# A hybrid decoder layer on one core: additions moved behind the next step, loads reordered at the ends of column pairs

## The chip, the cores and the metric

One core of a Trainium2 chip runs the whole program. The metric is the time of one execution in microseconds on the device: the median of the runs, before the change 1211.42 us over three (1210.86 to 1213.59). The core's engines are TensorE (PE in the profile), VectorE (DVE), ScalarE (ACT), GpSimd (POOL) and SyncE (SP). Each has its own queue of instructions, which it works off in order; semaphores tie the queues together. DMAs are issued from the queues of SyncE, GpSimd and ScalarE and carried out by 16 DMA engines.

## The reference, cut to what matters

256 tokens and 16 meta tokens in front of them go through one layer of width 2048. It has two halves, a mixer and a feed-forward block, and only the second is touched by the change:

```python
h = h + mix                                      # mixer: retention and mLSTM heads, then w_out
u = rmsnorm(h, norm_ffn)
up = causal_dwconv(u @ w_up, ffn_conv_w, ffn_conv_b)   # 2048 -> 2 x 5632, three taps
gate, val = jnp.split(up, [FFN_DIM], axis=-1)
h = h + (silu(gate) * val) @ w_down              # 5632 -> 2048
h = rmsnorm(h, norm_final)
return h[:, N_META:]
```

Everything is float32.

## The kernel before

**Products in three parts.** Each matrix operand is split into a rounded part `hi` (ScalarE's copy) and a rest `lo` (VectorE's subtraction, raw minus hi), and a product is hi·hi + hi·lo + lo·hi. So each raw weight tile costs one ScalarE copy (L141, L768), one VectorE subtraction (L143, L770) and three matmuls per pair of operands. Five `whi` and five `wlo` buffers stand between the splits and TensorE.

**Weights.** Raw weight tiles come through four buffers, `wraw0` and `wraw1` with two each (`raw_home`, L119). The loads of the mixer and the up-projection go round through them by a counter (`load_raw`, L122): two loads to side 0, two to side 1. The loads of the down-projection name their side themselves and do not move the counter.

**The feed-forward block** runs in two halves of the hidden width (from L759 on). A half has 44 up-projections (176 weight loads over both halves), the convolution, the gate, and then its part of the down-projection, summed into `hn`, the output tile of two token blocks `tt` of 128 rows by four column blocks `b` of 512.

**The down-projection of a half** takes the four column blocks as two pairs, `b` = 0 and `b` = 2. A pair has 11 steps `q`, each over 256 hidden rows. Steps 0, 9 and 10 are plain (`product`): two weight tiles, 24 matmuls of 512 columns. Steps 1 to 8 are fast (`seven`, L826): a scheme of seven products for a 2 by 2 block, 21 matmuls. Its raw tile of four quarters is in `left`, two buffers in the memory of `hT`, used in turn. VectorE forms one difference tile `ta` from it (L832); a precomputed sum `tb` comes by a load of its own. Both have their places in two buffers of `wraw1` (`sums_home`). Then four groups are split and multiplied. The quarter `raw[:, 0]` and the sum are read from `kept`, which was made in DRAM by accumulating DMAs (`Early`) during the up-projection.

In the last pair (second half, `b` = 2; `final`) three of the fast steps are done as plain ones, the order is 0, 1, 6, 2, 7, 3, 4, 5, 8, 9, 10, and the last normalization is woven in: `squares` on ScalarE, `times_gain` on GpSimd with the gain vector `gfin`, paced by a small GpSimd instruction (L855) that reads the step's sum.

**The end of a pair.** At the last fast step (8), `share` (L867 to L884) combines the four shared accumulators and adds the results to `hn`: GpSimd issues four accumulating DMAs (`onto`), to blocks (0, b), (1, b), (0, b+1), (1, b+1) in this order, and the last of them is `shared`. After step 10, four more accumulators `cs` are copied by ScalarE to tiles `x` (L1003) and added by VectorE to the same blocks of `hn` (L1004), after the DMA to the block has landed. The last of those copies is `emptied`; the splits of the next pair's first fast step are queued behind it.

**Order.** The framework draws up each engine's queue ahead of time: of what is ready at a moment, the work that comes first in the program. `issue_after(i)` puts work behind instruction `i` on that engine's queue, without waiting for it to end. SyncE's loads of the down-projection all go through `load` (L906), which chains them in program order by `begun`. GpSimd's sum loads are queued behind `shared`. At a pair's end SyncE's order is: step 8's tile, the next pair's step 1 (asked for at step 7), step 10's plain tiles, the next pair's step 0, its step 2 (both asked for at step 9).

Of the kernel before, what the change touches and what calls it, by code (L numbers as in the profile page):

```python
# [13 lines left out]
ALU = mybir.AluOpType  # L14
# [72 lines left out]
def trunk(ctx: ExitStack, tc: tile.TileContext, io, out: bass.AP):  # L87
# [28 lines left out]
    last_load = None  # L116
    loads = paced = 0

# [640 lines left out]
    for half in range(2):  # L759
# [66 lines left out]
        def seven(b, q, cs, ps, first, last, after, norm):  # L826
# [7 lines left out]
            for w, to in (  # L834
# [8 lines left out]
                with tc.issue_after(after.ins) if first and after else nullcontext():  # L843
                    copied, _ = split(hi[:, :n, :], lo[:, :n, :], w)
                for i, (m, o, begin, _) in enumerate(to):
# [4 lines left out]
            if norm:  # L850

                with tc.issue_after(copied.ins):
                    for g in norm:
                        squares(*g)
                reached = nc.gpsimd.tensor_tensor(out=junk[:, 0:1], in0=tb[:, 0, 0:1], in1=tb[:, 0, 0:1], op=ALU.add)  # L855
                with tc.issue_after(reached.ins):
                    for tt, _, c0, c1 in norm:
                        times_gain(tt, c0, c1)

        def block(tt, b):  # L860
# [41 lines left out]

        homes, raws = {}, {}
        begun = shared = None

# [10 lines left out]
        def load_seven(b, q):  # L916
# [9 lines left out]
        def load_sum(b, q):  # L926

            tb = sums_home[1][:, FAST.index(q) % 2, :][:, None, :]
            with tc.issue_after(shared.ins) if shared else nullcontext():
                nc.gpsimd.dma_start(tb[:, 0, :], early[b, half * NQD + q].kept[:, 1, :])  # L930
            homes[b, q] = homes[b, q], sums_home[0], tb
# [4 lines left out]
        lag = 4  # L936
        gains = []
        emptied = None
        for b in (0, 2):
# [18 lines left out]
            for q in steps:  # L958
                if q in fast:
                    due = []  # L960
                    if final and q != fast[0]:
                        due, gains = gains[:1], gains[1:]
                    seven(b, q, cs, ps, q == fast[0], q == fast[-1], emptied, due)
                    if q == fast[-1]:
# [18 lines left out]
                else:  # L983
# [5 lines left out]
                    if q == 8:  # L989
                        load_plain(b, 10, 1)  # L990
                    if b == 0:
                        if q == 7:
                            load_seven(2, 1)
                        elif q == 9:
                            load_plain(2, 0, 0)
                            load_seven(2, 2)
            for j in range(2):
                for n, tt in enumerate(range(2)):
                    c = (b + j) * 512
                    if not final:  # L1000

                        x = x_tile((4, 3, 1, 0)[2 * j + n])
                        emptied = nc.scalar.copy(x, cs[tt, j])  # L1003
                        nc.vector.tensor_tensor(out=block(tt, b + j), in0=block(tt, b + j), in1=x, op=ALU.add)  # L1004
                        if half == 1:
# [116 lines left out]
```

## Time and profile before

| | |
|---|---|
| median of three runs | 1211.42 us (1210.86 to 1213.59) |
| the profiled execution | 1212.01 us, its span 1210.2 us |
| TensorE busy | 1198.8 us, 99% |
| VectorE busy | 951.6 us, 79% |
| ScalarE busy | 713.4 us, 59% |
| DMA | 278.50 MB, mean 230 GB/s |
| first down-projection | TensorE from 718.8 to about 833.5 us |
| second down-projection | TensorE from 1087.2 us to the end |

Times in the views are microseconds from the span's start. A row of the timeline has the start, the length, the engine, the line, the operation, what it writes and reads, how many instructions it sums up, and in brackets how long the engine was idle before and what ended that. SPq and POOL rows of DMAs show the issue, not the transfer. Rows of the windows view have, per stretch, the stretch and its length, then for PE, PEld, DVE, ACT and POOL the busy time with the number of instructions that start or run in it, then the granted TensorE clock, the DMA engines' busy share and GB/s. Matmuls are pipelined, so the distance from start to start tells more than the length of one.

### The profile page before, as it was taken

The numbers are of one execution on the slowest core, as the hardware profiler recorded it, in microseconds if no ns is written. First come the engines' busy times: TensorE is split into PE (matmuls) and PEld (weight loads), VectorE is DVE, ScalarE is ACT, GpSimd is POOL, SyncE is SP. The second block draws the span as 40 slices with busy tenths as digits, with TensorE's granted clock in tenths as the row PEclk, the third lists the DMA queues.
The fourth block names the chain that finished last, engine by engine and source line by source line (L and its number), as shares of the span: only waits on it lengthen the run. The fifth ranks groups of instructions, "written<-read, shape, count | busy, mean of one in ns | idle before, by whom it ended". The sixth has DMA issues, their size and how long they took to land.

```text
span 1210.2 us, 23069 instructions
## 1 busy us (share of the span) xinstructions
PE 1198.8 (99%) x8947; PEld 1150.3 (95%) x8947; DVE 951.6 (79%) x1390; ACT 713.4 (59%) x973; POOL 258.7 (21%) x349
## 2 busy tenths in 40 slices
PE   9999999999999999999999999999999999999997
PEld 9999999999999999999999998878999999998786
DVE  8877778766775867788889779897877777778896
ACT  8657746656556556555555557665655555556673
POOL 0100022223231322233132100101133223300132
PEclk9999999999999999999999999999999999999999
DMA  7765677878786977788887757777888778847955
GB/s 278 263 224 159 203 235 210 254 217 238 209 244 208 260 223 222 238 256 227 237 229 224 233 181 261 229 249 228 271 228 252 240 222 237 221 161 265 291 195 183
DMA packets 102366, 278.50 MB, mean 230 GB/s; under 512 B 16432, under 2 KB 20656, under 8 KB 102128
## 3 DMA queue, kind: packets, MB, share of 16 engines
q1 hardware_dynamic: 84016, 239.06, 58.0%
q0 software_dynamic: 17664, 37.11, 17.5%
q8 instruction: 70, 1.15, 0.4%
q10 hardware_dynamic: 576, 0.85, 0.2%
q14 instruction: 40, 0.33, 0.1%
HBM read 268.59 MB, written 42.47 MB: 257 GB/s over the span
## 4 chain that ended last, share of the span: by engine, by line
PE 95%; DMA 2%; DVE 1%; ACT 0%; issue 0%; SPq 0%; DVEq 0%; ACTq 0%
PE mmps L150 25%; PE mmps L153 25%; PE mmps L151 25%; PE atps L821 2%; PE mmps L849 2%; PE atps L822 2%; PE atps L824 2%; PE mmps L846 2%; PE mmps L847 2%; PE atps L846 1%; PE atps L847 1%; PE atps L849 1%; DMA wraw<-in_wu 1%; DVE wlo L770 1%; DMA hT<-kept 1%; PE atps L444 1%
## 5 line engine op out<-in xcount | busy, mean ns | idle before, releaser
L141 ACT CAST whi<-wraw 128x1024 fp32r<-128x1024 f32 x346 | 361.8, 1049 | 334.0 <-PE mmps L151 221.6
L143 DVE TENSOR_TENSOR wlo<-wraw,whi 128x1024 fp32r<-128x1024 f32 x346 | 430.2, 1246 | 79.0 <-ACT whi L141 74.8
L150 PE MATMUL mmps<-uh,whi 128*128 128x258 f32 x1408 | 345.3, 283 | 0.6 <-ACT whi L141 0.6
L151 PE MATMUL mmps<-ul,whi 128*128 128x258 f32 x1408 | 345.0, 281 | 0.0
L151 PEld LDWEIGHTS mmps<-ul,whi 128*128 128x128 f32 x1408 | 266.6, 189 | 0.1
L150 PEld LDWEIGHTS mmps<-uh,whi 128*128 128x128 f32 x1408 | 265.3, 188 | 0.9 <-ACT whi L141 0.8
L150 PE MATMUL mmps<-xh,whi 128*128 128x272 f32 (+2 forms) x864 | 219.7, 287 | 0.0
L151 PE MATMUL mmps<-xl,whi 128*128 128x272 f32 (+2 forms) x864 | 218.2, 285 | 0.0
L153 PE MATMUL mmps<-uh,wlo 128*128 128x258 f32 x1408 | 197.9, 283 | 0.0
L153 PEld LDWEIGHTS mmps<-uh,wlo 128*128 128x128 f32 x1408 | 181.7, 189 | 0.0
L151 PEld LDWEIGHTS mmps<-xl,whi 128*128 128x128 f32 x864 | 162.6, 188 | 0.0
L150 PEld LDWEIGHTS mmps<-xh,whi 128*128 128x128 f32 x864 | 162.5, 188 | 0.1
L210 POOL TENSOR_TENSOR pace<-whi 128x1 f32<-128x1 f32 x87 | 52.2, 600 | 429.9 <-ACT whi L141 411.8
L153 PE MATMUL mmps<-xh,wlo 128*128 128x272 f32 (+2 forms) x864 | 126.8, 285 | 0.0
L153 PEld LDWEIGHTS mmps<-xh,wlo 128*128 128x128 f32 x864 | 114.5, 188 | 0.0
L697 DVE TENSOR_TENSOR cu<-mmps,rstd 128x258 f32<-128x258 f32 x88 | 37.6, 427 | 72.9 <-PE mmps L153 72.2
L770 DVE TENSOR_TENSOR wlo<-hT,whi 128x1024 fp32r<-128x1024 f32 x58 | 69.3, 1218 | 3.5 <-ACT whi L768 3.5
L768 ACT CAST whi<-hT 128x1024 fp32r<-128x1024 f32 x58 | 59.3, 1049 | 15.7 <-DMA hT<-kept 5.3
L768 ACT CAST whi<-wraw 128x1024 fp32r<-128x1024 f32 (+1 forms) x58 | 46.6, 835 | 35.5 <-DVE wraw L832 17.7
L151 PE MATMUL mmps<-mixl,whi 128*128 128x258 f32 x256 | 63.1, 283 | 0.0
L150 PE MATMUL mmps<-mixh,whi 128*128 128x258 f32 x256 | 62.5, 283 | 0.0
L770 DVE TENSOR_TENSOR wlo<-wraw,whi 128x1024 fp32r<-128x1024 f32 (+1 forms) x58 | 53.2, 952 | 1.5 <-ACT whi L768 0.5
(272 smaller groups left out, 1768.3 us busy)
## 6 DMA issues: line engine op xcount, KB each, us to landing
wraw<-in_wu SPq DMA_DIRECT2D x176, 512.0 KB, 4.5
wraw<-in_wi SPq DMA_DIRECT2D x108, 512.0 KB, 4.5
wraw<-in_wo SPq DMA_DIRECT2D x32, 512.0 KB, 5.4
wraw<-in_wd SPq DMA_DIRECT2D x30, 512.0 KB, 5.6
kept<-in_wd SPq DMA_DIRECT2D x29, 512.0 KB, 6.8
kept<-in_wd POOLq DMA_DIRECT2D x58, 256.0 KB, 6.7
hT<-in_wd SPq DMA_DIRECT2D x29, 512.0 KB, 4.9
kept<-kept POOLq DMA_DIRECT2D x29, 256.0 KB, 5.4
```

The costliest lines, as they stand in the source:

```text
L141: nc.scalar.copy(hi, raw)
L143: nc.vector.tensor_tensor(out=lo, in0=raw, in1=hi.bitcast(F32), op=ALU.subtract)
L150: nc.tensor.matmul(ps, hi[:, k, :], xh(kk), start=kk == first, stop=False)
L151: nc.tensor.matmul(ps, hi[:, k, :], xl(kk), start=False, stop=False)
L153: nc.tensor.matmul(ps, lo[:, k, :], xh(kk), start=False, stop=kk == last)
L210: with tc.issue_after(nc.gpsimd.tensor_tensor(out=pace, in0=x, in1=x, op=ALU.add).ins):
L697: evacuated = nc.vector.tensor_tensor(out=u, in0=ps[:, :NQ], in1=rstd2, op=ALU.mult)
L768: copied = nc.scalar.copy(hi, x)
L770: return copied, nc.vector.tensor_tensor(out=lo, in0=x, in1=hi.bitcast(F32), op=ALU.subtract)
L846: nc.tensor.matmul(o, sh[:, f, m, :], hi[:, i, :], start=begin, stop=False)
L847: nc.tensor.matmul(o, sl[:, f, m, :], hi[:, i, :], start=False, stop=False)
L849: nc.tensor.matmul(o, sh[:, f, m, :], lo[:, i, :], start=False, stop=end)
```

## The change

Six edits, all but one in the down-projection:

1. The additions of `cs` to column block `b + 1` at the end of each half's first pair are not made there: they are put on a list and made behind the next pair's first fast step. Those to block `b` and those of the second pair stay.
2. The next pair's step 1 is no longer asked for at step 7, but at step 9 behind step 0's plain tiles. Its step 2, asked for there too, is issued by GpSimd, behind `shared`, and not by SyncE.
3. In the last pair the sums of steps 3 to 5 are loaded by SyncE through `load`.
4. `gfin` is loaded in four quarters at steps 3 to 6 of the second half's first pair, behind that step's sum load, and not as a whole when the down-projection begins.
5. The pacing instruction of GpSimd writes a scratch of its own, `pace`, in place of `junk`.
6. The counter of the weight loads starts at 3 in place of 0, so that the sides come in the order 1, 0, 0, 1, 1 and not 0, 0, 1, 1.

```diff
-    loads = paced = 0
+    loads, paced = 3, 0
...
-                    copied, _ = split(hi[:, :n, :], lo[:, :n, :], w)
+                    copied, parted = split(hi[:, :n, :], lo[:, :n, :], w)
...
-                reached = nc.gpsimd.tensor_tensor(out=junk[:, 0:1], in0=tb[:, 0, 0:1], in1=tb[:, 0, 0:1], op=ALU.add)
+                reached = nc.gpsimd.tensor_tensor(out=pace, in0=tb[:, 0, 0:1], in1=tb[:, 0, 0:1], op=ALU.add)
...
+            return parted
...
-            nc.gpsimd.dma_start(gfin, io["gfin"])
...
-            load(raw[:, 2:4, :], io["wd7"][b // 2, half * NQD + q][:, 2:4, :])
-            load(raw[:, 1, :], io["wd7"][b // 2, half * NQD + q][:, 1, :])
-            load(raw[:, 0, :], early[b, half * NQD + q].kept[:, 0, :])
+            w = io["wd7"][b // 2, half * NQD + q]
+            parts = ((raw[:, 2:4, :], w[:, 2:4, :]), (raw[:, 1, :], w[:, 1, :]), (raw[:, 0, :], early[b, half * NQD + q].kept[:, 0, :]))
+            for to, src in parts:
+                if (b, q) == (2, 2):
+                    with tc.issue_after(shared.ins):
+                        nc.gpsimd.dma_start(to, src)
+                else:
+                    load(to, src)
...
-            with tc.issue_after(shared.ins) if shared else nullcontext():
-                nc.gpsimd.dma_start(tb[:, 0, :], early[b, half * NQD + q].kept[:, 1, :])
+            kept = early[b, half * NQD + q].kept[:, 1, :]
+            if half == 1 and b == 2 and q > 2:
+                load(tb[:, 0, :], kept)
+            else:
+                with tc.issue_after(shared.ins) if shared else nullcontext():
+                    summed = nc.gpsimd.dma_start(tb[:, 0, :], kept)
...
-                    seven(b, q, cs, ps, q == fast[0], q == fast[-1], emptied, due)
+                    done = seven(b, q, cs, ps, q == fast[0], q == fast[-1], emptied, due)
+                    if q == fast[0]:
+                        with tc.issue_after(done.ins):
+                            while later:
+                                later.pop(0)()
...
+                    if (half, b) == (1, 0) and q in range(3, 7):
+                        cols = slice((q - 3) * 512, (q - 2) * 512)
+                        with tc.issue_after(summed.ins):
+                            nc.gpsimd.dma_start(gfin[:, cols], io["gfin"][:, cols])
                     if b == 0:
-                        if q == 7:
+                        if q == 9:
+                            load_plain(2, 0, 0)
                             load_seven(2, 1)
-                        elif q == 9:
-                            load_plain(2, 0, 0)
                             load_seven(2, 2)
...
-                        nc.vector.tensor_tensor(out=block(tt, b + j), in0=block(tt, b + j), in1=x, op=ALU.add)
+                        later.append(lambda to=block(tt, b + j), x=x: nc.vector.tensor_tensor(out=to, in0=to, in1=x, op=ALU.add))
+                        if j == 0 or b == 2:
+                            later.pop(0)()
```

More of the change, by code (lines that the diff above doesn't have):

```diff
@@ L903, in trunk @@
         homes, raws = {}, {}
-        begun = shared = None
+        begun = shared = summed = None
         def load(to, src):
@@ L920, in load_seven @@
             turn = 1 - turn
-            load(raw[:, 2:4, :], io["wd7"][b // 2, half * NQD + q][:, 2:4, :])
-            load(raw[:, 1, :], io["wd7"][b // 2, half * NQD + q][:, 1, :])
-            load(raw[:, 0, :], early[b, half * NQD + q].kept[:, 0, :])
+            w = io["wd7"][b // 2, half * NQD + q]
[6 more added lines that the diff above has]
+                    load(to, src)
             homes[b, q] = raw
         def load_sum(b, q):
+            nonlocal summed
             tb = sums_home[1][:, FAST.index(q) % 2, :][:, None, :]
-            with tc.issue_after(shared.ins) if shared else nullcontext():
-                nc.gpsimd.dma_start(tb[:, 0, :], early[b, half * NQD + q].kept[:, 1, :])
+            kept = early[b, half * NQD + q].kept[:, 1, :]
[4 more added lines that the diff above has]
+                    summed = nc.gpsimd.dma_start(tb[:, 0, :], kept)
             homes[b, q] = homes[b, q], sums_home[0], tb
@@ L936, in trunk @@
         lag = 4
-        gains = []
+        gains, later = [], []
         emptied = None
```

## The prediction

> **What bounds the kernel now.** First the page's busy line and its slices, then TensorE (PE) by windows, its timeline where it is not steady, and the chain of waits there.
>
> ```profile
> span 1210.2 us, 23069 instructions
> PE 1198.8 (99%) x8947; PEld 1150.3 (95%) x8947; DVE 951.6 (79%) x1390; ACT 713.4 (59%) x973; POOL 258.7 (21%) x349
> 780.00:800.00 20.00, 20.00 (x87) 16.10 (x86) 19.94 (x21) 12.67 (x15) 2.16 (x4) 1.00 0.74 241
> 800.00:820.00 20.00, 19.03 (x78) 14.04 (x77) 18.05 (x18) 13.37 (x16) 1.08 (x2) 1.00 0.57 206
> ...
> 814.45 0.63 PE L849 MATMUL mmps<-wlo,sh 128*128 128x512 f32 x2
> 815.87 0.51 PE L846 MATMUL atps<-whi,sh 128*128 128x512 f32 x1 [0.79 <-ACT whi L768]
> ...
> 834.86 1.13 PE L153 MATMUL mmps<-uh,wlo 128*128 128x258 f32 x8
> 836.54 0.39 PE L150 MATMUL mmps<-uh,whi 128*128 128x258 f32 x1 [0.56 <-ACT whi L141]
> ...
> 1128.73 0.86 PE L849 MATMUL atps<-wlo,sh 128*128 128x512 f32 x3
> 1129.78 0.50 PE L846 MATMUL mmps<-whi,sh 128*128 128x512 f32 x1 [0.18 <-ACT whi L768]
> ...
> 807.71 8.29 DMA hT<-kept
> 826.73 8.63 DMA wraw<-in_wu
> ```
>
> TensorE is the bound: 1198.8 of 1210.2 us, at a granted clock of 1.00 in both windows. A change of this kind can only gain where TensorE waits, and in the stages it touches there are three such places. A steady 20 us window starts 87 matmuls, so a 512-column one goes out every 0.23 us. **Stall A**, the end of the second pair in the first half: 78 starts, 9 fewer, 9 x 0.23 = 2.1 us; the largest piece is the step from 814.45 (two matmuls, so the next was due at 814.92) to 815.87. **Stall B**, the second weight tile of the second up-projection: eight 258-column matmuls from 834.86 take 0.12 us each, so the next was due at 835.82 and came at 836.54; with the one slow start after it 0.8 us. **Stall C**, the end of the first pair in the second half: due at 1129.43, came at 1129.78; with the slow start 0.45 us. Together 3.3 us: all that this change can gain there, 0.28% of the span.
>
> The chain shows what ended last: for A the load of `kept` (part of step 8's raw tile), 8.29 us from issue to landing; for B a weight load that was issued at 826.73 and took 8.63 us. Behind A stands VectorE (DVE), busy 19.94 of 20 us in the steady window: it has no slack in the run of fast steps, so what it is late at the start of a pair is still missing at its end.
>
> **The change part by part.** *The deferred additions.* VectorE at the switch from pair 0 to pair 2, first half; ScalarE's copy (ACT); SyncE's loads (SPq); GpSimd's (POOL):
>
> ```profile
> 771.38 1.22 DVE L832 TENSOR_TENSOR wraw<-hT 128x1024 f32<-128x1024 f32 x1
> ...
> 774.13 1.29 DVE L1004 TENSOR_TENSOR hn<-hn,x 128x512 f32<-128x512 f32 x2
> 776.24 0.69 DVE L1004 TENSOR_TENSOR hn<-hn,x 128x512 f32<-128x512 f32 x1 [0.82 <-DMA hn<-x]
> 778.27 0.69 DVE L1004 TENSOR_TENSOR hn<-hn,x 128x512 f32<-128x512 f32 x1 [1.34 <-DMA hn<-x]
> 778.88 2.35 DVE L770 TENSOR_TENSOR wlo<-hT,whi 128x1024 fp32r<-128x1024 f32 x2
> 781.15 1.82 DVE L770 TENSOR_TENSOR wlo<-wraw,whi 128x1024 fp32r<-128x1024 f32 x2
> 782.89 1.22 DVE L832 TENSOR_TENSOR wraw<-hT 128x1024 f32<-128x1024 f32 x1
> ...
> 816.12 1.23 DVE L832 TENSOR_TENSOR wraw<-hT 128x1024 f32<-128x1024 f32 x1 [1.82 <-DMA hT<-kept]
> ```
>
> ```profile
> 776.22 0.59 ACT L1003 COPY x<-atps 128x512 f32<-128x512 f32 x1 [1.08 <-DMA hn<-x]
> 753.78 1.46 SPq L909 DMA_DIRECT2D hT<-in_wd  x2
> 755.34 0.41 SPq L909 DMA_DIRECT2D hT<-kept  x1
> ...
> 761.35 3.19 SPq L909 DMA_DIRECT2D wraw<-in_wd  x4
> 764.59 0.99 SPq L909 DMA_DIRECT2D hT<-in_wd  x2
> 765.63 0.72 SPq L909 DMA_DIRECT2D hT<-kept  x1
> 780.13 0.33 SPq L909 DMA_DIRECT2D hT<-in_wd  x1
> ...
> 769.43 1.79 POOL L930 DMA_DIRECT2D wraw<-kept  x2
> ```
>
> The third and fourth addition (L1004, column block 1) wait 0.82 + 1.34 = 2.16 us for the shared sums to land; the next pair's splits stand behind them. Deferring these two takes 2.16 us of idle and 1.3 us of work from in front of step 1 and puts the work, by then free of a wait, behind it: alone a gain of 2.16 us for VectorE, enough for all of A.
>
> *The loads of steps 1 and 2.* Before, step 1's tile goes out at 753.78 to 755.34, long ahead, so its difference (L832) is formed at 771.38 in VectorE's slack. In the change it stands on SyncE behind the two plain loads, exactly where step 2's stands now (764.59, 765.63). What that place costs, and how full the DMA engines are:
>
> ```profile
> DMA to landing us min/median/max: 5.0/5.3/5.5
> ...
> DMA to landing us min/median/max: 3.6/10.6/12.8
> ```
>
> ```profile
> q1 hardware_dynamic: 988, 3.06, 50.9%
> q0 software_dynamic: 736, 1.57, 39.0%
> wraw<-kept POOLq DMA_DIRECT2D x2, 256.0 KB, 10.0
> 764.00:768.00 4.00, 4.00 (x19) 3.23 (x18) 3.50 (x6) 2.10 (x2) 1.31 (x2) 1.00 1.00 279
> 772.00:776.00 4.00, 4.00 (x19) 3.20 (x18) 3.03 (x4) 2.62 (x4) 0.00 (x0) 1.00 1.09 274
> ```
>
> The first of these lines is for raw tiles issued at 753 to 756, the second at 763 to 781: 5.3 us against up to 12.8. The last part, issued at 765.63, lands at 778.4. So step 1 becomes whole at 778.4 instead of before 771.4. VectorE after: two additions to 775.4; idle until ScalarE, whose copy at 776.22 is still held by a shared sum, has made the first split (about 777.8); split to 778.9; the difference, newly here, to 780.1; two splits of 1.14 each to 782.3; the small one to 783.0; the two deferred additions to 784.3. Before it was at this point at 782.89. So it starts the run 1.4 us **later**, not earlier: 2.16 us of idle go, but some 2.4 us (775.4 to 777.8) take their place, and 1.14 us of work come in. From there nothing is idle until A's 1.82 us wait, so A grows by 1.4 us.
>
> Step 2's tile (1 MB in three DMAs) goes to GpSimd's queue behind the shared sums. The engines are full there (share 1.00 and 1.09 at 279 and 274 GB/s), so its megabyte takes 1.05/0.28 = 3.7 us, by which the two sum loads behind it (10.0 us now, from 769.43) are later too: about 783, just when VectorE wants the first at 782.3. Bounds: 0, and 2.1 us: at half that rate the megabyte takes 7.5 us and the sum comes at 786.7, 4.4 us late, of which the difference and one split of step 2 (2 x 1.14 us) can fill 2.3 where the order of the queues allows. I take 0, nearest to these rows. [...]
>
> *The load counter from 3.* The four weight buffers are two of each side. The first half's last tile is the 237th load (9 + 108 + 32 + 88 in the loops' order); with the counter from 0 the second half starts on the second of one side. SyncE issued the load freed by plain step 9's second tile at 823.65, ahead of the one TensorE needs second, whose buffer came free with step 10's:
>
> ```profile
> 823.65 0.33 SPq L127 DMA_DIRECT2D wraw<-in_wu  x1
> 826.73 0.33 SPq L127 DMA_DIRECT2D wraw<-in_wu  x1
> ```
>
> From 3 on, the first two loads get the two buffers that step 9 frees, and the second needed one is issued 826.73 - 823.65 = 3.1 us sooner. The lateness it has to cover is 0.72 us: B goes, 0.8 us. 2.4 us are to spare; if a slower landing eats them, B stays.
>
> *The gain vector in quarters.* Now 1 MB on GpSimd's queue as the second half's pairs begin; VectorE idles there:
>
> ```profile
> 1093.67 1.23 DVE L770 TENSOR_TENSOR wlo<-hT,whi 128x1024 fp32r<-128x1024 f32 x1 [2.20 <-ACT whi L768]
> 1095.96 1.22 DVE L832 TENSOR_TENSOR wraw<-hT 128x1024 f32<-128x1024 f32 x1 [1.07 <-DMA hT<-kept]
> ```
>
> Taking it away brings up to 2.20 + 1.07 = 3.3 us of lead, more than C. Against it, each quarter in steps 3 to 6 costs 0.26/0.28 = 0.9 us of the engines, in a stage that is not full (share 0.74 in the like window). Bounds: -0.45 (C gone) and +0.9 (the last quarter meets step 9's loads and delays step 8). I take -0.45.
>
> *The rest.* GpSimd's own scratch frees it from a wait on ScalarE's `junk`, but its next work, the gain, needs the same squares: 0. The sum loads of the last pair that move to SyncE wait there for the buffer that a split frees; behind them stands a plain load that is used after two more steps: 0; if that cover went, about one step's 4.9 us (21 matmuls). At the last pair's start the same loads as in the first half come late, but a plain step (24 matmuls, 5.6 us of TensorE for 2.3 us of VectorE) follows the first fast one: bounds 0 and 2.1 us as above, and I take 0.4.
>
> **Sum:** -0.8 (B) - 0.45 (C) + 1.4 (A) + 0.4 (last pair) = +0.55 us. The profiled execution took 1212.0 us (its span of 1210.2 and 1.8 us around it), so 1212.55. The median of the runs shown is 0.6 us below it: **1211.9 us**.
>
> **The rivals.** (1) *It does what it says*: step 1's tile lands by 775, and the 2.16 us of idle simply go. For it: every wait it removes is in the rows. Against it: the 12.8 us. Then A, B and C go, 3.3 us: 1208.1. (2) *The sums come late, and it is slower*: GpSimd's queue serves step 2's megabyte first, in both halves, and TensorE waits for the step's last product. It decides if the first sum load lands after 783.0 in the first half. [...] Price: the forecast, 1 us more in the first half (half the bound of 2.1, since SyncE issues nothing from 766 to 780.13 and shares the engines only at its ends) and 2.1 in place of 0.4 in the last pair, where step 6's plain loads share them throughout: +0.55 + 1.0 + 1.7 = +3.25: 1214.7. For it: share 1.00; against: what SyncE issued has landed by 778.4. (3) *A was chance*: its load took 8.29 us where 5.3 is usual; without its 1.82 us wait A ends at 2.1 + 1.4 - 1.8 = 1.7: -0.8 - 0.45 - 0.4 + 0.4 = -1.25, 1210.2.
>
> **How the numbers follow.** Forecast 0.50, rival 1 0.14, rival 2 0.20, rival 3 0.16. A measurement of this kernel tells 0.2%, 2.4 us, from no change. Faster by more: rival 1 and a little of rival 3, 0.18. Slower: rival 2 and the forecast's upper tail, 0.22. The rest 0.60. The range goes from near rival 1 to rival 2: 1208.3 to 1215.0, a little past rival 2, since its 2.1 us may hit both halves. The forecast's own is 1210.5 to 1213.5.
>
> **What would show it.** B right: the step from the first to the second weight tile of the second up-projection is 2.9 us. C right: no wait at the end of that pair, and none of VectorE at its start. A right: the difference of step 1 (L832) starts after 778 and a stall of 2.5 us or more stands before 835; wrong if it starts before 775. Rival 2: a wait of ScalarE for `wraw<-kept` just after a pair's switch. All of it is wrong if TensorE loses time outside these stages.

## The result, and the profile after

The changed kernel takes 1217.8 us (median of 6 runs, 1215.82 to 1221.14) beside 1211.26 us for the kernel before in the same session (6 runs, 1210.19 to 1213.59). The ratio is 1.0054, with a 95% interval of 1.0038 to 1.0070: slower by 6.5 us. The prediction said 1211.9 and at most 1215.0, so it was wrong. The profiled execution took 1217.84 us, 5.8 more than before.

The page of the changed kernel, its span and TensorE's share; beside 1210.2 and 1198.8 before:

```profile
span 1216.1 us, 23075 instructions
PE 1200.8 (99%) x8947; PEld 1149.9 (95%) x8947; DVE 950.7 (78%) x1390; ACT 713.1 (59%) x973; POOL 262.7 (22%) x355
```

The windows of the changed kernel, then the two of the kernel before that the prediction did not show:

```profile
780.00:800.00 20.00, 18.21 (x76) 13.63 (x75) 19.95 (x22) 12.23 (x15) 1.61 (x3) 1.00 0.68 231
800.00:820.00 20.00, 19.29 (x82) 14.91 (x81) 18.77 (x19) 12.50 (x15) 1.61 (x3) 1.00 0.73 258
...
1120.00:1140.00 20.00, 20.00 (x87) 15.88 (x86) 18.57 (x20) 12.03 (x15) 2.85 (x4) 1.00 0.68 231
1140.00:1160.00 20.00, 18.42 (x76) 13.67 (x75) 12.71 (x15) 11.28 (x15) 5.56 (x8) 1.00 0.99 317
```

```profile
1120.00:1140.00 20.00, 19.82 (x86) 15.64 (x85) 18.82 (x21) 12.54 (x14) 4.31 (x7) 1.00 0.83 274
1140.00:1160.00 20.00, 20.00 (x87) 15.84 (x86) 17.32 (x18) 13.06 (x18) 3.63 (x5) 1.00 0.91 289
```

They are read at 0.23 us for a matmul and 87 matmuls to a steady window. In the second pair of the first half 11 + 5 matmuls are missing, 3.7 us, where 9 were missing before: the larger part now lies at the start of the pair. In 1120 to 1140 nothing is missing: C is gone in this execution. In 1140 to 1160, the start of the last pair, 11 are missing, 2.5 us, where none was. The two losses lie at the two switches from the first pair to the second, the place that the edit on the loads touches.

Both traces hold 8947 matmuls, so the n-th of one can be set beside the n-th of the other. Judged by when it starts, the changed kernel is then behind the kernel before by:

| time in the kernel before | behind by |
|---|---|
| 20 | 0.7 us |
| 718.8, first product of the first down-projection | 0.7 us |
| 780, start of its second pair | 0.7 us |
| 810 | 4.0 us |
| 833, end of that pair | 3.4 us |
| 840, second up-projection, past stall B | 2.6 us |
| 1120, first pair of the second half | 2.6 us |
| 1145, the last pair's first step | 2.4 us |
| 1160 | 4.8 us |
| 1195, end of the last pair | 5.4 us |
| the end | 5.8 us |

So the first half costs 2.8 us and B gives 0.8 back; the start of the last pair costs 2.4 us and its end 0.6. The old stall at the end of the first half's second pair has not grown. A new loss of 3.3 us has come at that pair's start, and 0.5 us less is lost at its end.

VectorE at both switches in the changed kernel (timeline; line numbers are one higher than before, and more below the edits):

```profile
779.52 1.23 DVE L833 TENSOR_TENSOR wraw<-hT 128x1024 f32<-128x1024 f32 x1 [4.34 <-DMA hT<-kept]
780.66 1.29 DVE L1025 TENSOR_TENSOR hn<-hn,x 128x512 f32<-128x512 f32 x2
781.86 2.35 DVE L771 TENSOR_TENSOR wlo<-hT,whi 128x1024 fp32r<-128x1024 f32 x2
...
785.87 1.29 DVE L1025 TENSOR_TENSOR hn<-hn,x 128x512 f32<-128x512 f32 x2
787.08 1.22 DVE L833 TENSOR_TENSOR wraw<-hT 128x1024 f32<-128x1024 f32 x1
...
819.56 1.22 DVE L833 TENSOR_TENSOR wraw<-hT 128x1024 f32<-128x1024 f32 x1 [1.12 <-DMA hT<-kept]
...
1151.03 1.23 DVE L833 TENSOR_TENSOR wraw<-hT 128x1024 f32<-128x1024 f32 x1 [4.14 <-DMA hT<-kept]
```

The difference of step 1 (L833) waits 4.34 and 4.14 us for the last part of step 1's tile. The two additions (L1025 here) to column block 0 come *behind* it, and so do all four splits. VectorE reaches the difference of step 2 at 787.08, where it was at 782.89 before and 784.3 was predicted. By 0.7 us the whole trace is behind already; what is left is 3.5 us and 2.1 us. The wait for step 8's `kept` at the end of the pair is 1.12 us (819.56), 1.82 before. The tile's transfers in the first half (issues at 765.6 to 767.0, from issue to landing), beside 5.0 to 5.5 us before:

```profile
DMA to landing us min/median/max: 9.8/11.3/12.4
```

TensorE's waits behind it, in the changed kernel:

```profile
789.50 0.50 PE L847 MATMUL mmps<-whi,sh 128*128 128x512 f32 x1 [1.11 <-ACT whi L769]
...
795.78 0.50 PE L847 MATMUL mmps<-whi,sh 128*128 128x512 f32 x1 [0.65 <-ACT whi L769]
...
1154.65 0.74 PE L850 MATMUL atps<-wlo,sh 128*128 128x512 f32 x2 [0.75 <-DVE wlo L771]
...
1158.78 0.50 PE L850 MATMUL atps<-wlo,sh 128*128 128x512 f32 x1 [0.66 <-DVE wlo L771]
...
1200.26 0.50 PE L822 MATMUL atps<-whi,mh 128*128 128x512 f32 x1 [0.37 <-ACT whi L142]
```

The sign that the prediction named for its rival 2 is there too, a wait of ScalarE for a sum just after the switch, and the sum comes after the 783.0 that was to decide:

```profile
783.99 0.62 ACT L769 CAST whi<-wraw 128x512 fp32r<-128x512 f32 x1 [2.11 <-DMA wraw<-kept]
```

VectorE has the next work on this sum, and it is busy with other work until then (no idle time in its rows from 779.52 to 787.08), so in the first half the wait is covered. Whether the sums cost anything is asked by the second run below.

### The profile page after: what moved, and what is told of

Its sections match the earlier page's. It is cut to its first block, busy times and chain, and to the rows that moved or that the text cites. A ratio compares the mean times of both kernels' runs of the same rounds, so it can differ in the third digit from the quotient of the medians.

```text
span 1216.1 us, 23075 instructions
## 1 busy us (share of the span) xinstructions
PE 1200.8 (99%) x8947; PEld 1149.9 (95%) x8947; DVE 950.7 (78%) x1390; ACT 713.1 (59%) x973; POOL 262.7 (22%) x355
## 4 chain that ended last, share of the span: by engine, by line
PE 95%; DVE 2%; DMA 2%; ACT 1%; issue 0%; SPq 0%; DVEq 0%; ACTq 0%
PE mmps L151 25%; PE mmps L154 25%; PE mmps L152 25%; PE mmps L847 2%; PE mmps L848 2%; PE atps L822 2%; PE atps L825 2%; PE atps L823 2%; PE mmps L850 2%; PE atps L850 1%; PE atps L848 1%; PE atps L847 1%; DVE wlo L771 1%; DMA hT<-kept 1%; PE atps L445 1%; DMA wraw<-in_wd 1%
## 5 line engine op out<-in xcount | busy, mean ns | idle before, releaser
L771 DVE TENSOR_TENSOR wlo<-hT,whi 128x1024 fp32r<-128x1024 f32 x58 | 70.3, 1236 | 2.3 <-ACT whi L769 2.3
L771 DVE TENSOR_TENSOR wlo<-wraw,whi 128x1024 fp32r<-128x1024 f32 (+1 forms) x58 | 55.4, 989 | 1.7 <-PE mmps L850 0.7
```

The lines of the kernel that those rows point to most:

```text
L771: return copied, nc.vector.tensor_tensor(out=lo, in0=x, in1=hi.bitcast(F32), op=ALU.subtract)
```

## The experiments

Four theories are told apart. **L**: the loss is step 1's tile, late at the switch. **S** (the prediction's rival 2): the loss is the sum loads, late behind step 2's megabyte on GpSimd. Later **P**: what is left of A, and C, come from step 8's tile, which is queued behind plain step 9's megabyte; and **G**: the place of step 2 on GpSimd helps. The times of the kernel before in the four sessions were 1211.2, 1211.4, 1211.9 and 1212.2 us, so the ratios compare better than the times.

### Step 1 early again

The changed kernel with this block as before:

```diff
-                        if q == 9:
-                            load_plain(2, 0, 0)
+                        if q == 7:
                             load_seven(2, 1)
+                        elif q == 9:
+                            load_plain(2, 0, 0)
                             load_seven(2, 2)
```

> The changed kernel with the next pair's step 1 asked for at step 7 again; step 2 stays on GpSimd's queue. Theory L (the late tile of step 1 costs the time: VectorE's difference stands in front of its queue and waits 4.3 us for it): the tile lands before 762, no wait of 4 us before L833, VectorE reaches the difference of step 2 at 783 +- 1 and not at 787.1, and the time falls to 1209.5 to 1211.5. Rival S (the sum loads behind step 2's megabyte on GpSimd's queue are late and hold VectorE and TensorE): the time stays at 1215 or more.

1210.51 us, ratio 0.9993 (0.9984 to 1.0002): 7.3 us come back with one load moved, while step 2 stays on GpSimd. L holds and S falls. VectorE in this run:

```profile
781.97 1.22 DVE L833 TENSOR_TENSOR wraw<-hT 128x1024 f32<-128x1024 f32 x1
...
814.94 1.23 DVE L833 TENSOR_TENSOR wraw<-hT 128x1024 f32<-128x1024 f32 x1 [1.52 <-DMA hT<-kept]
```

It is at the difference of step 2 at 781.97, 0.9 us earlier than before the change. Yet a wait of 1.52 us for step 8's `kept` stands at the end of the pair, as it did before (1.82).

### Step 2 back on SyncE, step 1 still late

```diff
-                if (b, q) == (2, 2):
+                if False:
```

> The changed kernel with step 2's tile on SyncE again, behind the late step 1; the sums no longer have it ahead of them. Theory L: the 4.3 us wait stays, so 1216 to 1219, and the sums land 3 to 4 us sooner without effect in the first half; in the last pair, where a sum that lands at 1156.3 is followed by a ScalarE split at 1156.4, up to 1.5 us may come back. Rival S: 1212 to 1213.

1218.28 us, ratio 1.0062 (1.0046 to 1.0079). Taking step 2 off GpSimd mends nothing that the times show: S falls once more. For the last pair alone this is less sure. In the traced execution of this run, at 1215.86 us the fastest of its four (up to 1219.63), VectorE waits 4.37 us for the tile there too, yet only 2 matmuls are missing from 1140 to 1160 where 11 were.

### The edit on the loads alone

The kernel before with the edit on the loads of steps 1 and 2 and nothing else:

```diff
-                        if q == 7:
+                        if q == 9:
+                            load_plain(2, 0, 0)
                             load_seven(2, 1)
-                        elif q == 9:
-                            load_plain(2, 0, 0)
                             load_seven(2, 2)
...
+                if (b, q) == (2, 2):
+                    with tc.issue_after(shared.ins):
+                        nc.gpsimd.dma_start(to, src)
+                else:
+                    load(to, src)
```

> The kernel before with the edit on the loads of steps 1 and 2 alone. Theory L: it costs by itself what the change costs and B and C besides, 6.5 + 1.2: 1217 to 1220. Rival D (the deferral is the cost): 1210 to 1213.

1219.42 us, ratio 1.0070 (1.0055 to 1.0085). This one edit makes the whole loss; whether it makes more than the whole change, the overlapping intervals leave open. Its wait is the same as in the changed kernel, and all four additions follow it:

```profile
779.59 1.22 DVE L832 TENSOR_TENSOR wraw<-hT 128x1024 f32<-128x1024 f32 x1 [4.29 <-DMA hT<-kept]
780.73 2.49 DVE L1009 TENSOR_TENSOR hn<-hn,x 128x512 f32<-128x512 f32 x4
```

### Without the edit on the loads

The changed kernel with both diffs of the first two runs together, so that both loads are as before; the deferral, the gain vector, the counter, the scratch and the last pair's sums stay.

> The changed kernel without its edit on the loads of steps 1 and 2 at all; the deferred additions, the quarters of the gain, the sums on SyncE, the scratch and the counter stay. Theory L: the deferral now gains its 2.16 us of idle, stalls A, B and C go: 1208 to 1210. Rival S: the same time, and e1 well above it. If the deferral itself is the cost (rival D), it stays above 1213.

1211.43 us, ratio 1.0003 (0.9994 to 1.0012): a miss. The rest of the change, which was to bring 1 to 3 us, brings nothing that the times show. So the deferral was run by itself.

### The deferral alone

The kernel before, and:

```diff
-                        nc.vector.tensor_tensor(out=block(tt, b + j), in0=block(tt, b + j), in1=x, op=ALU.add)
+                        later.append(lambda to=block(tt, b + j), x=x: nc.vector.tensor_tensor(out=to, in0=to, in1=x, op=ALU.add))
+                        if j == 0 or b == 2:
+                            later.pop(0)()
```

> The kernel before with the additions to column block b + 1 behind the next pair's first fast step, and nothing else. As the prediction had it, this alone is worth 2.16 us to VectorE and all of stall A: 1209.3. Theory W, formed on the run with both tiles back (its split of step 1 waited 1.41 us for ScalarE): the wait for the shared sums only passes from VectorE's additions to ScalarE's copy, behind which the splits are queued: VectorE reaches the difference of step 2 between 782.4 and 783.9, as the 782.89 before, and the time is 1211.4.

1212.05 us beside 1211.89, ratio 0.9999 (0.9991 to 1.0008): theory W. ScalarE and VectorE at the switch of this run:

```profile
776.50 0.59 ACT L1008 COPY x<-atps 128x512 f32<-128x512 f32 x1 [1.35 <-DMA hn<-x]
776.98 2.00 ACT L768 CAST whi<-hT 128x1024 fp32r<-128x1024 f32 x2
```

```profile
778.06 2.36 DVE L770 TENSOR_TENSOR wlo<-hT,whi 128x1024 fp32r<-128x1024 f32 x2 [2.81 <-ACT whi L768]
...
783.28 1.22 DVE L832 TENSOR_TENSOR wraw<-hT 128x1024 f32<-128x1024 f32 x1
```

VectorE no longer waits 0.82 + 1.34 us for shared sums, but 2.81 us for ScalarE. ScalarE's last copy writes an `x` tile that a shared sum's DMA still reads, so it waits for that DMA (1.35 us), and the next pair's splits are queued behind the copy. The wait passed to the other engine. A gain of up to 1.1 us stays possible by the interval. In the traced execution, 1.4 us under the median, 83 matmuls start from 800 to 820 where 78 did, so A is smaller there; whether that is the deferral or the varying landing of step 8's tile is not shown.

### The difference behind the additions

The changed kernel, step 1 late, and VectorE's difference of the pair's first fast step queued behind the two additions that stay at the switch:

```diff
-            nc.vector.tensor_tensor(out=ta, in0=raw[:, 0:1, :].to_broadcast([P, 2, 512]), in1=raw[:, 1:3, :], op=ALU.subtract)
+            with tc.issue_after(added.ins) if first and added else nullcontext():
+                nc.vector.tensor_tensor(out=ta, in0=raw[:, 0:1, :].to_broadcast([P, 2, 512]), in1=raw[:, 1:3, :], op=ALU.subtract)
```

> The changed kernel, but VectorE's difference of the new pair's step 1 is queued behind the two additions to column block b that stay at the switch; its tile is as late as in the changed kernel. Theory O (part of the cost is the order of VectorE's queue: the two additions stand behind a difference that waits 4.3 us for its tile): they are made inside the wait, VectorE is 1.3 us further at each switch (the first half's difference of step 2 at 785.8 in place of 787.1), and the time is 1.3 to 2.6 us lower than the changed kernel's: 1215.2 to 1216.5. Rival (the late tile alone sets it, the order costs nothing): 1217.8 as in the changed kernel.

1216.25 us, ratio 1.0039 (1.0024 to 1.0053), 1.5 permille or 1.8 us under the changed kernel's 1.0054; the two intervals overlap, so the times do not settle it. The rows go the way of theory O:

```profile
773.89 1.28 DVE L1026 TENSOR_TENSOR hn<-hn,x 128x512 f32<-128x512 f32 x2
778.26 1.23 DVE L834 TENSOR_TENSOR wraw<-hT 128x1024 f32<-128x1024 f32 x1 [3.08 <-DMA hT<-kept]
...
785.24 1.22 DVE L834 TENSOR_TENSOR wraw<-hT 128x1024 f32<-128x1024 f32 x1
```

The additions now lie inside the wait, and the difference of step 2 comes at 785.24 in place of 787.08. Half of these 1.84 us is only an earlier trace: the first product of the down-projection starts at 718.58 here and at 719.48 in the changed kernel. So 0.9 us is gained, not the 1.3 expected. Set matmul by matmul beside the kernel before, TensorE loses 2.1 and 1.6 us at the two switches, where the changed kernel lost 2.8 and 2.4. The place of the two additions thus made about 1.5 of 5.2 us there, and the late tile with the work that is still behind it the rest. In this one execution the gain is lost again later: C is back, and the end of the last pair costs 1.4 us in place of 0.6.

### Late in the last pair only

The changed kernel with step 1 early in the first half and late in the second:

```diff
-                        if q == 9:
+                        if q == 7 and half == 0:
+                            load_seven(2, 1)
+                        elif q == 9:
                             load_plain(2, 0, 0)
-                            load_seven(2, 1)
+                            if half == 1:
+                                load_seven(2, 1)
                             load_seven(2, 2)
```

> The changed kernel, but step 1 of the second pair is asked for at step 7 again in the first half and stays late in the second, so that only the last pair has it late. Beside the run with step 1 early in both (1210.5): by the forecast's term for the last pair, 0.4 us more, 1210.9; by the stalls in the trace of the changed kernel, 2.4 us at the last pair's start and 0.5 at its end, less the 0.6 that the early run has there itself: 2.3 more, 1212.8; if the two halves share the cost evenly, 3.6 more, 1214.1.

1213.96 us, ratio 1.0013 (1.0004 to 1.0022). Against the 0.9993 with step 1 early in both halves that is 2.0 permille, 2.4 us, near the 2.3 of the middle expectation; the first half has the remaining 4.1 permille, 5 us. The intervals make both rough to a microsecond or two; the traces, matmul by matmul, give 2.4 and 4.1 us. Its window at the last pair's start:

```profile
1140.00:1160.00 20.00, 18.37 (x77) 13.79 (x76) 14.49 (x15) 12.71 (x17) 3.18 (x4) 1.00 0.88 291
```

Ten matmuls are missing, 2.3 us: the plain step that follows covers nothing of it.

### The counter alone

```diff
-    loads = paced = 0
+    loads, paced = 3, 0
```

> The kernel before with the load counter from 3 and nothing else. By the forecast's term B, TensorE's late start on the second weight tile of the second up-projection goes and nothing else moves: 0.8 us faster, about 1210.4 beside 1211.2. Rival: the counter also shifts which side each weight load of the mixer and the first up-projection takes, and that is paid for at the kernel's start or at the switch to the first down-projection: no change, 1211.2, with the stall at 836 gone all the same.

1211.13 us, ratio 0.9996 (0.9987 to 1.0005): too small for the times to tell. The timeline of TensorE shows that stall B is gone:

```profile
835.36 1.12 PE L153 MATMUL mmps<-uh,wlo 128*128 128x258 f32 x8
836.32 0.28 PE L150 MATMUL mmps<-uh,whi 128*128 128x258 f32 x1
```

Eight matmuls at 0.12 us end at 836.32, and there the second weight tile starts; it was 0.72 us late before.

### The gain vector in quarters alone

```diff
-            nc.gpsimd.dma_start(gfin, io["gfin"])
...
+                    if (half, b) == (1, 0) and q in range(3, 7):
+                        cols = slice((q - 3) * 512, (q - 2) * 512)
+                        with tc.issue_after(summed.ins):
+                            nc.gpsimd.dma_start(gfin[:, cols], io["gfin"][:, cols])
```

> The kernel before with the gain vector in four quarters at steps 3 to 6 and nothing else. By the forecast's term C: VectorE's waits of 2.20 and 1.07 us near 1093 to 1096 go, and with them the stall of 0.45 us at 1129.8: about 1210.75. Rival: the quarters meet the loads of steps 7 to 9 and step 8's tile is late in the second half as it is in the first: 0 to 0.9 us slower, 1211.2 to 1212.1.

1211.67 us, ratio 1.0003 (0.9994 to 1.0012): the times leave it open, and the trace goes with the rival. VectorE and TensorE near the end of that pair:

```profile
1094.39 1.23 DVE L832 TENSOR_TENSOR wraw<-hT 128x1024 f32<-128x1024 f32 x1 [3.26 <-DMA hT<-kept]
...
1127.98 1.23 DVE L832 TENSOR_TENSOR wraw<-hT 128x1024 f32<-128x1024 f32 x1 [0.43 <-DMA hT<-kept]
```

```profile
1127.39 0.63 PE L849 MATMUL mmps<-wlo,sh 128*128 128x512 f32 x2
1129.06 0.50 PE L846 MATMUL mmps<-whi,sh 128*128 128x512 f32 x1 [1.04 <-ACT whi L768]
```

VectorE idles 3.26 us at the pair's start, as long as before (2.20 + 1.07). Yet the tile is there sooner: the last part of it was issued at 1088.7 in both, and the difference starts at 1094.39 in place of 1095.96. The first split, which ran at 1093.67 before, now stands behind the difference, so at the difference of step 2 VectorE is only 0.25 us ahead (1099.88 beside 1100.13). At the end the next matmul was due at 1127.86 and came at 1129.06, 1.2 us late where it was 0.35 before: C has grown by 0.85 us.

### Step 9's loads behind step 8's tile

The run with step 1 early, and plain step 9's two tiles asked for behind step 8's:

```diff
-                    if q == 6:
-                        load_plain(b, 9, 0)
                     if q in range(1, 7):
                         load_seven(b, q + 2)
                         load_sum(b, q + 2)
+                    if q == 6:
+                        load_plain(b, 9, 0)
```

> The changed kernel with step 1's tile asked for at step 7 again, and plain step 9's two tiles asked for behind step 8's tile and not ahead of it. Theory P (what is left of stall A is the wait of VectorE for the last part of step 8's tile, which queues behind step 9's megabyte): that wait of 1.5 us goes in the first half, TensorE gains about 0.9 us in the first half beside the run with step 1 early (1210.5), and the time is 1209.6. Rival 3 of the prediction put the other way (the wait only takes up time that VectorE is ahead anyway, or step 9's tiles now come late in their turn): 1210.5 or above, with a wait of ScalarE for step 9's tile at about 820.

1208.78 us, ratio 0.9979 (0.9970 to 0.9988): faster than the kernel before and the changed one, and 0.8 us better than theory P expected. Its windows:

```profile
800.00:820.00 20.00, 20.00 (x88) 16.07 (x87) 19.88 (x20) 14.30 (x17) 1.21 (x3) 1.00 0.62 204
1120.00:1140.00 20.00, 20.00 (x88) 16.07 (x87) 18.39 (x20) 10.75 (x14) 6.27 (x9) 1.00 0.94 273
1140.00:1160.00 20.00, 20.00 (x88) 16.09 (x87) 17.40 (x17) 13.47 (x17) 2.09 (x3) 1.00 0.79 282
```

No matmul is missing: A and C are gone, and the last pair starts clean.

### The same with the kernel before, without and with the counter

The kernel before with the diff just shown and nothing else; then with the counter too:

```diff
-    loads = paced = 0
+    loads, paced = 3, 0
```

> The kernel before with plain step 9's two tiles asked for behind step 8's tile, and nothing else. Theory P (stalls A and C both come from step 8's tile, which queues behind step 9's megabyte): A's 2.1 and C's 0.45 us go without any of the change, B's 0.8 stays: 1208.9. Rival Q (VectorE is late from the pair's switch on, as the prediction said, and the deferral is needed with it): half of A stays, 1210.0.

1210.73 us, ratio 0.9990 (0.9981 to 0.9998).

> The kernel before with plain step 9's tiles behind step 8's tile and the load counter from 3. By theory P and term B together no stall is left in the down-projections: 1208.2, and not above the 1208.8 of the run that has the rest of the change too. By rival Q: 1209.3.

1210.15 us, ratio 0.9990 (0.9981 to 0.9999). Both stay short of what P gave: 1.2 us for the first in place of 2.5. Moving step 9's loads is not enough. A is mostly gone in both (0.5 and 0.3 us are left in the traces). C is gone in the first and still there in the second: the first row below was due at 1127.17. And in the first a stall stands at the last pair's start, whose releaser is again ScalarE's copy, held for 1.1 us by a shared sum (the second has one of 0.81 us there):

```profile
1127.59 0.50 PE L846 MATMUL mmps<-whi,sh 128*128 128x512 f32 x1 [0.25 <-ACT whi L768]
...
1141.92 0.51 PE L821 MATMUL atps<-whi,mh 128*128 128x512 f32 x1 [0.68 <-ACT x L1003]
```

So P holds for A and not for C.

### Which edit makes the rest

The 1208.8 us kernel once with step 2 on SyncE again, once with all four additions at the switch again:

```diff
-                if (b, q) == (2, 2):
+                if False:
```

> The run with step 1 early and step 9's loads behind step 8's tile (1208.8), but step 2 issued by SyncE again. Theory G (step 2's megabyte on SyncE runs beside the shared sums of the switch, and its place on GpSimd behind them is what spares the last pair): the sums land in 8 to 10 us instead of 6.3 to 8.8, ScalarE's copy waits about 1 us and TensorE stalls 0.8 to 1.0 us near 1141, as in the run with step 9's loads alone moved: 1209.7. Rival (the issuer makes no difference, the deferral alone does it): 1208.8, no stall near 1141.

1209.65 us, ratio 0.9981 (0.9972 to 0.9990).

```diff
-                        if j == 0 or b == 2:
-                            later.pop(0)()
+                        later.pop(0)()
```

> The run with step 1 early and step 9's loads behind step 8's tile (1208.8), but all four additions at the switch again. By theory G the last pair stays clean (no stall near 1141), and in the first half VectorE waits for one or two sums again and is 0.5 to 1.5 us later at the difference of step 2 than the 781.7 there; 0.3 to 0.5 us of stall A comes back near 812: 1209.2. Rival (the deferral does nothing anywhere): 1208.8. Rival (it is the deferral that spares the last pair): 1209.8 with the stall near 1141.

1208.97 us, ratio 0.9975 (0.9965 to 0.9985). Without the deferral nothing is lost that the times show, and no stall appears at 812. With step 2 on SyncE the ratio is 0.2 permille above that of the 1208.8 us kernel and 0.6 above that of the run without the deferral, 0.2 and 0.7 us, where theory G had 0.9. Nor is the loss where G put it: TensorE has no stall near 1141, and in the first half four matmuls are missing:

```profile
800.00:820.00 20.00, 19.64 (x84) 15.42 (x83) 19.89 (x21) 13.91 (x17) 1.07 (x2) 1.00 0.63 213
1140.00:1160.00 20.00, 20.00 (x87) 16.11 (x86) 16.28 (x16) 13.27 (x18) 3.23 (x3) 1.00 0.83 265
```

The intervals overlap, so the times do not settle whether G's edit gains; the windows are clear. The two runs with step 9's loads ahead and step 1 early, which differ in the place of step 2 alone, go the same way, 0.9993 on GpSimd and 1.0003 on SyncE, again with intervals that overlap. From issue to landing of the shared sums, first half and second, in the 1208.8 us kernel:

```profile
DMA to landing us min/median/max: 5.8/6.7/7.9
...
DMA to landing us min/median/max: 6.3/7.6/8.8
```

and with step 2 on SyncE, with VectorE's row in the first half:

```profile
DMA to landing us min/median/max: 7.9/8.2/9.4
...
DMA to landing us min/median/max: 9.1/9.5/11.0
```

```profile
778.09 2.36 DVE L771 TENSOR_TENSOR wlo<-hT,whi 128x1024 fp32r<-128x1024 f32 x2 [2.47 <-ACT whi L769]
...
783.31 1.22 DVE L833 TENSOR_TENSOR wraw<-hT 128x1024 f32<-128x1024 f32 x1
```

Behind the shared sums, step 2's megabyte lets them land 1.5 to 1.9 us sooner. Then, in the first half, neither ScalarE's copy nor VectorE's addition has to wait, wherever the additions stand; without the deferral VectorE makes all four in one go:

```profile
774.56 2.49 DVE L1026 TENSOR_TENSOR hn<-hn,x 128x512 f32<-128x512 f32 x4
...
781.63 1.22 DVE L833 TENSOR_TENSOR wraw<-hT 128x1024 f32<-128x1024 f32 x1
```

The waits for the shared sums that the deferral was to step around are removed there by this other edit at their source. In the second half one addition still waits 0.67 us. What spares TensorE at 1141 with step 2 on SyncE, where ScalarE's copies wait 0.94 and 1.45 us for shared sums, was not run by itself.

## Why the prediction was wrong, by its steps

**What bounds the kernel.** Right. TensorE's stalls are what moves the time, and the 3.3 us of A, B and C were there to be had: the 1208.8 us kernel has none of them. It is 2.5 us under the kernel before by its ratio, 1.5 to 3.6 by the interval.

**A, +1.4.** Right in sign and in cause (step 1's tile late by its place in SyncE's queue), wrong in size and in where it is lost. The first half costs 2.8 us in the traced execution; against the same change with step 1 early it is 4.1 us by the traces and about 5, to a microsecond or two, by the runs. The step that failed is the order assumed on VectorE: "two additions to 775.4; idle until ScalarE [...] has made the first split (about 777.8); split to 778.9; the difference". In the trace the difference comes first, and the two additions (0.6 us each) and the first split, which were ready, stand behind its wait of 4.34 us. Counted from the first product of the down-projection (718.82 and 719.48), the difference of step 1 starts as forecast, 60.0 us where 60.1 was given. The difference of step 2 comes at 67.6 in place of 65.5, 2.1 us late: the additions are 1.2 us of work and the first split 1.1. And "From there nothing is idle until A's 1.82 us wait, so A grows by 1.4 us" put the loss at the end of the pair; TensorE waits at once, in the first steps behind the switch. The experiment on the order got 0.9 of the 3.5 us of lateness back.

**The last pair, +0.4.** Wrong: 2.4 us by the run that is late only there. The cover named, "a plain step [...] follows the first fast one", doesn't help, because TensorE waits inside the fast step itself, for the splits that come behind the difference (0.75 and 0.66 us, released by L771). The second of them is the sum's split, which VectorE has behind the next fast step's difference (1156.90). The upper bound of 2.1 was near the truth. The choice of a value near the lower end was the error. How much of it the place of step 2 makes is open.

**B, -0.8.** Right: the stall of 0.72 us went with the counter alone, though the times can't tell it from no change.

**C, -0.45.** Gone in the changed kernel, but the edit named does not do it alone. "Taking it away brings up to 2.20 + 1.07 = 3.3 us of lead" came to 0.25 us with the quarters alone. They make C worse, by 0.85 us, near the upper bound of 0.9: the last part of step 8's tile, in flight beside the last quarter, took 8.5 us in place of 6.9, and VectorE waits for it. In the changed kernel VectorE's wait at the start of that pair is 1.59 us and C does not come; which of the other edits adds to the quarters was not run. That C goes by VectorE's lead fits the rows: with step 9's loads moved in the kernel before, the tile's wait at that start is 0.54 us in the run where C is gone and 1.21 us in the one where it is there (1.07 before).

**The deferral.** "alone a gain of 2.16 us for VectorE, enough for all of A": 0 as far as the times tell, twice over (ratio 0.9999 alone; nothing lost when it is taken from the fastest kernel), each to about 1 us. For VectorE it was no gain: the difference of step 2 came at 783.28, 782.89 before. The forecast itself saw ScalarE's copy "still held by a shared sum" and used it against the deferral only with step 1 late; here the copy holds the splits with step 1 early as well.

**Step 2 on GpSimd, 0, bounded by 0 and 2.1.** Wrong side, as far as the runs tell: three pairs of runs differ in this edit alone (step 1 late, step 1 early, and step 9's loads moved too), by 0.8, 1.0 and 0.2 permille in its favour, none of them clear of noise. The bounds left out a gain: that the shared sums, now ahead of the megabyte, would land sooner was not looked at. What moved was the order in which the transfers are issued (step 2's tile from 770.3 to 771.4, behind the shared sums, and from 764.6 to 765.6, among them, before), and with step 9's loads moved too the shared sums land 1.5 to 1.9 us sooner (medians of 6.7 and 7.6 us beside 8.2 and 9.5). The bound of 2.1, which the last pair's 0.4 was chosen under and which rival 2's price and the upper end of the range are built on, takes half the rate for the megabyte, which no run shows. In the changed kernel the two sum loads behind the megabyte take 12.0 us from issue in the first half, where they took 10.0, and 13.6 in the last pair, where they took 10.6; ScalarE takes the first at 783.99, with the trace 0.7 us behind, where the forecast had about 783 and half the rate 786.7.

**The sum.** By the steps as measured in the two traces, A +2.8, B -0.8, C -0.3, the last pair's start +2.4 and its end +0.6, the first 20 us of the execution +0.7 and the stretch behind the last pair's products +0.4 make the profiled 5.8. The first 20 us are not placed: the two traces start 128 and 123 matmuls there, the other runs 124 to 131. Nor is the last 0.4. The 0.6 at the last pair's end (the wait before 1200.26) ends with a weight load that took 7.1 us. It stands in the four traces with step 1 late and the last pair's sums on SyncE (0.4 to 1.4 us), not in the run on the loads alone nor in those with step 1 early. So the 0 for the sums on SyncE may hold only with step 1 early; that edit was not run alone.

**The rivals.** Rival 1 (it does what it says) was not what happened; what it left standing was step 9's loads. Rival 2 had the right sign with the wrong mechanism. The wait it named is there (2.11 us of ScalarE), but with step 1 early and the sums still behind step 2's megabyte the loss is gone. Rival 3, that A was chance, falls in the main: with step 9's loads ahead VectorE waits for step 8's `kept` in nine of eleven traced executions, and in none of the five where they stand behind it. The length of the wait does vary, from 0.37 to 1.82 us.

## What to carry to other kernels

A load that is moved later is costed by its landing beside everything that is issued around its new place (here 9.8 to 12.4 us in place of 5.0 to 5.5), and then by the whole queue behind the first instruction that needs it, ready work included (here two additions and a split behind a wait of 4.34 us). Before a wait is deferred on one engine, look whether a second engine waits for the same event, here through the buffer that the DMA still reads (2.81 us of waiting for ScalarE in place of 0.82 + 1.34 for the sums); if so, make the event earlier. And when the DMA engines are full (a share of 1.00 at the switch before the change, 764 to 768), ask of a change of queue in what order the transfers will start: here 256 KB sums that two engines wait for landed 1.5 to 1.9 us sooner ahead of a megabyte than beside it.

## What was not expected of the hardware

In the run with the edit on the loads alone, the granted clock of TensorE fell after a wait of 1.92 us. Windows of two microseconds, and the first matmul behind the wait:

```profile
782.00:784.00 2.00, 0.50 (x3) 0.06 (x1) 2.00 (x4) 0.73 (x2) 0.00 (x0) 1.00 0.04 14
784.00:786.00 2.00, 1.59 (x5) 1.30 (x6) 2.00 (x3) 1.78 (x2) 0.00 (x0) 0.81 0.24 78
786.00:788.00 2.00, 2.00 (x6) 1.57 (x5) 2.00 (x3) 0.00 (x0) 0.48 (x1) 0.50 0.91 280
788.00:790.00 2.00, 2.00 (x8) 1.58 (x8) 2.00 (x3) 1.53 (x3) 0.06 (x1) 0.83 0.81 284
```

```profile
784.41 0.74 PE L849 MATMUL atps<-wlo,sh 128*128 128x512 f32 x2 [1.92 <-DVE wlo L770]
```

Behind the 1.92 us of idle time the clock is 0.50 in the window from 786 to 788 and 0.81 and 0.83 in those beside it, and only six matmuls start from 786 to 788 where at 0.23 us each there is room for nearly nine. The same happened near 1158 after a wait of 2.08 us: 0.50 and six matmuls from 1158 to 1160. So these two stalls cost more than their length. This may be why this kernel, which lacks the other five edits, has a median 1.6 us above the changed one's (the intervals overlap), whose waits in the rows shown are 1.11 us at most, at a clock of 1.00 in all four windows; no run was made to tell it apart.
